# Low-rank decay and rate products of an RWKV-7 block: one cluster per token piece, the low-weight products on 64 rows each

## The chip, the cores and the metric

The kernel runs on one core of a Trainium2 chip. The metric is device time in microseconds (us) of one execution; of three executions of the kernel before, the median is 1004.59 us (1003.79 to 1004.99). Engines are named as the profile names them: PE is TensorE's matrix multiply, PEld its weight load, DVE is VectorE, ACT is ScalarE, POOL is GpSimd, SP issues most transfers.

## The reference, cut to what matters

One layer of a hybrid block works on 528 tokens (16 learned ones ahead of 512 real ones) of width 2048. One input projection has 65 tiles of 128 columns; they feed an RWKV-7 branch of 16 heads and a short convolution branch, and one output projection joins both. One of the 65 tiles holds two low-rank inputs of 64 columns: `wl` for the decay and `al` for the rate.

```python
Pr = Pr + (prev - Pr) * mu_shift[l]          # token shift
wl = Pr[..., 4*D_RWKV : 4*D_RWKV + 64]
al = Pr[..., 4*D_RWKV + 64 :]
w_raw = -softplus(-(w0[l] + tanh(wl) @ w_lora_up[l])) - 0.5
decay = exp(-exp(w_raw))
a = sigmoid(a0[l] + al @ a_lora_up[l])       # per channel, 1024 wide
```

Decay and rate enter the recurrence over time of every head. The kernel computes them for a pair of heads (128 channels) at a time, so there are eight pairs.

## The kernel before, in words

**Number format.** Products run in a rounded 32-bit form (`F32R`), and a 32-bit operand is split in two: a high part, which is a copy in that form, and a low part, which is the rest. A full product is high by high, high by low and low by high.

**The input projection as filler.** `mains` (from L493) is a generator that emits the projection's matmuls (L346) tile by tile, in the order of `plan`. Everything else is placed among them: `fill(ns)` (L564) draws projection matmuls until their estimated time has passed, then the next piece of other work is emitted. The order of PE's instructions is this order, written out by hand; on the other engines a planner orders them by estimated times and priorities. A projection weight comes by a transfer on SP (L166), is cast on ACT (L158) and its low part is made on DVE or POOL (L159).

**A pair.** `prepare(i)` (L640) does one pair: it loads and splits the pair's low-rank weights (`lora_up`, L602; `luh` high, `lul` low, each 128 rows by 2 by 128), calls `low_rank` for the decay argument `tz` (index 0) and then for the rate argument `ta` (index 1), and goes on to a running sum `cc` (L654), two exponentials `e` (L656, L658), the operands `ar` and `bk` (L661 to L678) and the matmuls `gram` (L694). Pairs are taken two at a time; after the second, `invert` solves a small triangular system for both.

**The low-rank input `la`.** `use_lora` (L395) makes it once: for each of the two inputs, rows 0 to 63 hold the high part and rows 64 to 127 the low part. The weights come from the host twice over, in rows 0 to 63 and again in rows 64 to 127. So one matmul of 128 rows, `hi[:, j]` by `la[:, j]`, gives the high weights times high and low part of the input together.

**`low_rank` (L578).** For each of two pieces of the tokens (0 to 272, and 272 to 528) it takes one PSUM bank from a pool of two (`pz`, tag `tz`, which `gram` and `invert` use as well), issues a matmul with the high weights (L584) and one with the low weights (L585), both over 128 rows, then one or two ACT instructions that apply tanh out of the bank (L588 and L589 for the first piece, L591 for the second), and calls `fill(FW["lora"])`, 2200 ns of projection matmuls. The order on PE for a pair is thus: decay piece 1, filler, decay piece 2, filler, rate piece 1, filler, rate piece 2, filler.

**Later.** The recurrence over nine chunks (`recur`, from L953) uses what is left of the projection as filler; then comes the output projection (L1256).

Of the kernel before, what the change touches and what calls it, by code (L numbers as in the profile page):

```python
# [9 lines left out]
F32 = mybir.dt.float32  # L10
F32R = mybir.dt.float32r
I32 = mybir.dt.int32
AF = mybir.ActivationFunctionType
ALU = mybir.AluOpType
# [4 lines left out]
P = 128  # L19
# [3 lines left out]
META = 16  # L23
L = SEQ + META
CH = 64
NCH = SEQ // CH + 1
LP = NCH * CH
# [15 lines left out]
FW = dict(  # L43
    evac=34, start=1062, lora=2200, gram=8000, gram_b=13500, gram2=5500, misc=2000, v=2000, vt=1000, solve=24500, more={0: 5500, 2: 2400},
    tr=3200, lev=3000, cp=4200, out=1500, begin=19500, p=2900, u=2900, s=5200, last=3700, mix=2600,
)
# [52 lines left out]
def hymba_kernel(ctx: ExitStack, tc: tile.TileContext, xt, xtok, front, w_in, w_out, pv, lup, cst, msk, gf, out):  # L99
    nc = tc.nc  # L100
# [18 lines left out]
    def col(off, i=0):  # L119
        return pvt[:, off + i : off + i + 1]  # L120
# [59 lines left out]
    la = cq.tile([P, 2, L], F32R, name="la")  # L180
    ones = xp.tile([P, P + 2], F32R, name="ones")
    omm = xp.tile([P, 33], F32, name="omm")
    hv = xp.tile([P, 6, 8], F32, name="hv")
# [3 lines left out]
    pz = ph1.enter_context(tc.tile_pool(name="pz", bufs=2, space=PSUM))  # L187
# [6 lines left out]
    def tr(name, dt=F32):  # L194
        return cq.tile([P, LP], dt, tag="tr", name=name, bufs=5)

    def tm(name):
        return tp.tile([P, LP], F32, tag="tm", name=name, bufs=3)
# [118 lines left out]
    with tc.issue_after(head):  # L317
        nc.vector.tensor_scalar(
            out=omm, in0=pvt[:, V_MU : V_MU + 33], scalar1=-1.0, scalar2=1.0, op0=ALU.mult, op1=ALU.add
        )  # L320
        for d, off in (
# [4 lines left out]
                out=d, in0=pvt[:, off : off + 8], scalar1=0.5, scalar2=None, op0=ALU.mult  # L326
            )
        nc.vector.tensor_scalar(
            out=hv[:, 4], in0=pvt[:, V_KA : V_KA + 8], scalar1=-0.5, scalar2=1.0, op0=ALU.mult, op1=ALU.add
# [37 lines left out]
    def shift_full(ps, m, name, dst):  # L367
        pr = tp.tile([P, L + 1], F32, tag="pr", name=f"pr_{name}", bufs=2)
        nc.gpsimd.memset(pr[:, 0:1], 0.0)
        scaled(FULL, ps, pr, -1)  # L370
        sh = tm(f"sh_{name}")[:, 0:L]
        nc.scalar.activation(sh, pr[:, 0:L], AF.Copy, scale=col(V_MU, m))
        for (a, b), d in dst:
            nc.vector.scalar_tensor_tensor(
                out=d, in0=pr[:, a + 1 : b + 1], scalar=omm[:, m : m + 1], in1=sh[:, a:b], op0=ALU.mult, op1=ALU.add
            )
# [13 lines left out]
    def gate(g, name):  # L390
        th = tm(f"th_{name}")[:, 0:SEQ]
        nc.scalar.activation(th, g, AF.Tanh, scale=0.5)
        nc.vector.scalar_tensor_tensor(out=g, in0=th, scalar=1.0, in1=g, op0=ALU.add, op1=ALU.mult)

    def use_lora(ps):  # L395
        pre = tm("lora_pre")[:, 0:L]
        shift_full(ps, 32, "lora", (((0, L), pre),))
        th = tr("lora_th")[0:64, 0:L]
        al = tr("lora_al")[0:64, 0:L]
        nc.scalar.activation(th, pre[0:64], AF.Tanh)  # L400
        nc.vector.tensor_copy(al, pre[64:128])
        for j, t in enumerate((th, al)):
            nc.scalar.copy(la[0:64, j], t)
            nc.vector.tensor_tensor(out=la[64:128, j], in0=t, in1=la[0:64, j].bitcast(F32), op=ALU.subtract)

    got = {}

# [3 lines left out]
    def use(what, i, ps):  # L411
        if what == "lora":
            use_lora(ps)
        elif what in ("k", "v"):
            t = cq.tile([P, LP], F32, tag=what, name=f"{what}{i}")
# [139 lines left out]
    def step():  # L555
        t = next(flow, None)
        if t is None:
            run_pending(float("inf"))
        else:
            clock[0] += t  # L560
            run_pending(clock[0])
        return t

    def fill(ns):  # L564
        while ns > 0:
            seen = len(ready)
            t = step()
            if t is None:
                return
            ns -= t  # L570
            if len(ready) > seen:
                ns += FW["evac"]
# [2 lines left out]
        while key not in ready:  # L575
            step()

    def low_rank(i, j, up, w0, name, pad):  # L578
        t = tr(name)
        nc.gpsimd.memset(t[:, META:CH], pad)  # L580
        hi, lo = up
        for a, b in ((0, 272), (272, L)):
            z = pz.tile([P, b - a], F32, tag="tz", name=f"{name}_{a}")
            nc.tensor.matmul(z, hi[:, j], la[:, j, a:b], start=True, stop=False)  # L584
            nc.tensor.matmul(z, lo[:, j], la[:, j, a:b], start=False, stop=True)  # L585
            with tc.high_priority(offset=AHEAD):
                if a == 0:
                    nc.scalar.activation(t[:, 0:META], z[:, 0:META], AF.Tanh, bias=w0, scale=0.5)  # L588
                    nc.scalar.activation(t[:, CH : 5 * CH], z[:, META:272], AF.Tanh, bias=w0, scale=0.5)  # L589
                else:  # L590
                    nc.scalar.activation(t[:, 5 * CH : LP], z, AF.Tanh, bias=w0, scale=0.5)  # L591
            fill(FW["lora"])
        return t


    def ahead():
# [2 lines left out]
    def c3(t):  # L599
        return t.rearrange("p (c s) -> p c s", s=CH)  # L600

    def lora_up(i):  # L602
        raw = cq.tile([P, 2, P], F32, tag="lur", name=f"lur{i}")
        hi = cq.tile([P, 2, P], F32R, tag="luh", name=f"luh{i}")
        lo = cq.tile([P, 2, P], F32R, tag="lul", name=f"lul{i}")
        nc.sync.dma_start(raw, lup[i])
        nc.scalar.copy(hi, raw)
        nc.vector.tensor_tensor(out=lo, in0=raw, in1=hi.bitcast(F32), op=ALU.subtract)
        return hi, lo

    def split(t, name, n):
# [2 lines left out]
        nc.scalar.copy(hi, t)  # L614
        nc.vector.tensor_tensor(out=lo, in0=t, in1=hi.bitcast(F32), op=ALU.subtract)
        return hi, lo

    heads = [(h, slice(64 * h, 64 * h + 64), slice(64 - 64 * h, 128 - 64 * h)) for h in range(2)]

    place = [(i % 2) * 4 + i // 2 for i in range(NPAIR)]  # L620
    dd = keep.tile([P, NCH, NPAIR], F32, name="dd")
# [18 lines left out]
    def prepare(i):  # L640
# [6 lines left out]
        up = lora_up(i)  # L647
        fill(FW["start"] if i else 6700)

        tz = low_rank(i, 0, up, hv[:, 0, i : i + 1], f"tz{i}", -1.0)  # L650
        ta = low_rank(i, 1, up, hv[:, 1, i : i + 1], f"ta{i}", 0.0)
        nc.gpsimd.tensor_scalar(out=tz, in0=tz, scalar1=1.0, scalar2=None, op0=ALU.add)
        cc = tr(f"cc{i}")
        nc.vector.tensor_tensor_scan(cc, smask.rearrange("p c s -> p (c s)"), tz, 0.0, op0=ALU.mult, op1=ALU.add)  # L654
# [8 lines left out]
            out=bk[:, :, 0], in0=c3(k), scalar=hv[:, 2, i : i + 1], in1=c3(te), op0=ALU.mult, op1=ALU.mult  # L663
# [3 lines left out]
            out=ta, in0=ta, scalar1=hv[:, 3, i : i + 1], scalar2=hv[:, 4, i : i + 1], op0=ALU.mult, op1=ALU.add  # L667
        )
        nc.vector.scalar_tensor_tensor(
            out=ar[:, :, 0], in0=c3(k), scalar=col(V_KK, i), in1=e1[:, :, 0:CH], op0=ALU.mult, op1=ALU.mult  # L670
# [8 lines left out]
            out=ar[:, 1:NCH, 1], in0=c3(r), in1=e1[:, 1:NCH, 1 : CH + 1], op=ALU.mult  # L679
        )  # L680
        nc.vector.scalar_tensor_tensor(
            out=r, in0=r, scalar=hv[:, 5, i : i + 1], in1=ta[:, CH:LP], op0=ALU.mult, op1=ALU.mult
# [41 lines left out]
        zs = ((zn, 0, 288), (ze[0][0:2, P : P + 288], 288, LP))  # L724
# [54 lines left out]
        def sub(x, r0, c0, dims):  # L779
            return bass.AP(tensor=x.tensor, offset=x.offset + r0 * 16 + c0, ap=[list(x.ap[0])] + dims)  # L780

        for m in (2, 4, 8):
            for b in range(16 // (2 * m)):
# [4 lines left out]
                    out=pq,  # L788
                    in0=sub(d, o, o + m, [[16, m], [0, m], [1, m]]),
                    in1=sub(y, o + m, o + m, [[0, m], [1, m], [16, m]]),  # L790
                    op=ALU.mult,
                )
                nc.vector.tensor_reduce(
                    out=tq.rearrange("p (i j) -> p i j", i=m), in_=pq, op=ALU.add, axis=AX.X
                )
                nc.vector.tensor_tensor(
                    out=pq,
                    in0=sub(y, o, o, [[16, m], [0, m], [1, m]]),
                    in1=bass.AP(tensor=tq.tensor, offset=tq.offset, ap=[list(tq.ap[0]), [0, m], [1, m], [m, m]]),
                    op=ALU.mult,  # L800
# [274 lines left out]
    for i in range(0, NPAIR, 2):  # L1075
        invert([prepare(i), prepare(i + 1)])
# [155 lines left out]
    def here(t, n):  # L1232
        return xa[t][:, n * 512 : (n + 1) * 512] if n < 2 else xb[n - 2][:, t]
# [99 lines left out]
    for half in range(2):  # L1333
        o = 28 * half
        for g in range(4):
            b = o + 4 + 4 * g
# [50 lines left out]
    z = {}  # L1387
# [55 lines left out]
    with tc.manual_schedule(engines={mybir.EngineType.DVE, mybir.EngineType.Activation, mybir.EngineType.Pool}):  # L1443
# [16 lines left out]
        for part in range(2):  # L1460
            cols = slice(256 * part, 256 * part + 256)
            for jj in range(8):
                hi, lo = right[(1, "M2", jj // 2), jj % 2]
# [4 lines left out]
            h = here(1, 2)[:, cols]  # L1468
# [70 lines left out]
```

## Time and profile before

| what | value |
|---|---|
| median of three executions | 1004.59 us |
| profiled execution, its own time | 1003.5 us |
| its span, first to last instruction | 1001.6 us |
| granted TensorE clock, mean | 0.997 of full speed |
| PE busy | 991.5 us (99%) |
| DVE, ACT, POOL busy | 679.7, 394.5, 273.2 us |
| low-rank matmuls | 64 (8 pairs, 2 inputs, 2 pieces, 2 weight parts) |

A row of the timeline gives the start, the time, the engine, the line, what is written and read, the array tile (rows by columns, as in 128\*128), the moving operand's shape and how many like instructions were merged in the row. Matmuls are pipelined: a duration of 0.28 us is the time until a result is out, while the next matmul starts about 0.12 us after. What a matmul costs in a dense stream is therefore the distance from its start to the next start. The rows "PEld" are weight loads, which run beside the matmul before them.

### The profile page before, as it was taken

To read this page: it belongs to the slowest core of one execution; us is meant where nothing else is said; L and a number is where in the kernel's file an instruction comes from. 1 tells how busy PE (TensorE), PEld (TensorE's weight loads), DVE (VectorE), ACT (ScalarE), POOL (GpSimd) and SP (SyncE) were. 2 spreads that over 40 slices of the span, in tenths; PEclk is the share of its full clock that TensorE was granted. 3 is DMA by queue.
4 is the path that set the end of the run, shared out by engine and by line. 5 is a ranking of instruction groups with operands and counts; after the bars stand their busy time and mean duration, and the time that the engine had idled before them with its cause. 6 is when DMAs were issued, how large, how long until landed. Compare 5 with 4: busy or idle time off the path is not lost.

```text
span 1001.6 us, 23672 instructions
## 1 busy us (share of the span) xinstructions
PE 991.5 (99%) x9723; PEld 913.1 (91%) x9723; DVE 679.7 (68%) x1247; ACT 394.5 (39%) x729; POOL 273.2 (27%) x284
## 2 busy tenths in 40 slices
PE   9999999999999999999999999999999999999996
PEld 8999999999998999998999998989889898888885
DVE  7777865586775569654669654245555697997897
ACT  7553423344323434322434322223232435546454
POOL 0122524234222423233423232223332333001001
PEclk9999999999999999999999999999999999999998
DMA  9426586546675364854263855868674698797654
GB/s 332 144 84 152 126 219 159 153 128 143 154 185 168 99 167 101 216 158 119 85 173 96 224 143 166 321 201 249 203 227 101 171 268 212 187 304 188 160 127 168
DMA packets 185036, 174.82 MB, mean 175 GB/s; under 512 B 121568, under 2 KB 142816, under 8 KB 184416
## 3 DMA queue, kind: packets, MB, share of 16 engines
q1 hardware_dynamic: 182336, 164.40, 56.8%
q0 software_dynamic: 2304, 8.39, 4.9%
q8 instruction: 76, 1.25, 0.5%
q10 hardware_dynamic: 288, 0.52, 0.1%
q14 instruction: 32, 0.26, 0.1%
HBM read 136.92 MB, written 36.35 MB: 173 GB/s over the span
## 4 chain that ended last, share of the span: by engine, by line
PE 95%; DVE 3%; issue 1%; DMA 0%; ACT 0%; DVEq 0%; POOL 0%; ACTq 0%
PE ps_k L346 9%; PE ps_v L346 9%; PE ps_h L346 9%; PE ps_r L346 9%; PE ps_C L346 9%; PE ps_g L346 9%; PE ps_B L346 9%; PE ps_gc L346 9%; PE M L1256 5%; PE P L1256 4%; PE g L694 2%; PE Q L1256 2%; DVE o L1227 1%; PE ps_lora L346 1%; PE zs L1019 1%; PE rz L967 1%
## 5 line engine op out<-in xcount | busy, mean ns | idle before, releaser
L159 POOL TENSOR_TENSOR w<-wr,w 128x512 fp32r<-128x512 f32 x119 | 173.1, 1455 | 367.5 <-ACT w L158 316.3
L158 ACT CAST w<-wr 128x512 fp32r<-128x512 f32 x252 | 153.1, 619 | 287.2 <-PE ps_C L346 48.9
L159 DVE TENSOR_TENSOR w<-wr,w 128x512 fp32r<-128x512 f32 x133 | 98.2, 744 | 107.8 <-ACT w L158 107.5
L346 PE MATMUL ps_k<-xh,w 128*128 128x272 f32 (+1 forms) x512 | 95.3, 284 | 0.0
L346 PE MATMUL ps_v<-xh,w 128*128 128x256 f32 (+1 forms) x512 | 95.3, 284 | 0.0
L346 PE MATMUL ps_r<-xh,w 128*128 128x258 f32 (+1 forms) x512 | 94.9, 281 | 0.0
L346 PE MATMUL ps_h<-xh,w 128*128 128x256 f32 (+1 forms) x512 | 94.2, 283 | 0.0
L346 PE MATMUL ps_C<-xh,w 128*128 128x256 f32 (+1 forms) x512 | 93.1, 281 | 0.0
L346 PE MATMUL ps_g<-xh,w 128*128 128x256 f32 (+1 forms) x512 | 91.5, 280 | 0.0
L346 PE MATMUL ps_B<-xh,w 128*128 128x512 f32 x256 | 83.9, 395 | 0.0
L346 PE MATMUL ps_gc<-xh,w 128*128 128x512 f32 x256 | 81.3, 392 | 0.0
L346 PEld LDWEIGHTS ps_k<-xh,w 128*128 128x128 f32 x512 | 80.0, 188 | 0.4
L346 PEld LDWEIGHTS ps_v<-xh,w 128*128 128x128 f32 x512 | 80.0, 188 | 0.3
L346 PEld LDWEIGHTS ps_h<-xh,w 128*128 128x128 f32 x512 | 79.3, 188 | 0.9 <-issue 0.2
L346 PEld LDWEIGHTS ps_r<-xh,w 128*128 128x128 f32 x512 | 79.9, 188 | 0.1
L346 PEld LDWEIGHTS ps_C<-xh,w 128*128 128x128 f32 x512 | 79.2, 188 | 0.6
L346 PEld LDWEIGHTS ps_g<-xh,w 128*128 128x128 f32 x512 | 78.7, 188 | 0.3
L346 PE MATMUL ps_k<-xl,w 128*128 128x272 f32 (+1 forms) x256 | 72.6, 284 | 0.0
L346 PE MATMUL ps_v<-xl,w 128*128 128x272 f32 (+1 forms) x256 | 72.5, 283 | 0.0
L346 PE MATMUL ps_r<-xl,w 128*128 128x258 f32 (+1 forms) x256 | 72.2, 282 | 0.0
L346 PE MATMUL ps_g<-xl,w 128*128 128x258 f32 (+1 forms) x256 | 72.0, 281 | 0.0
L346 PE MATMUL ps_C<-xl,w 128*128 128x258 f32 (+1 forms) x256 | 71.8, 280 | 0.0
(321 smaller groups left out, 2256.7 us busy)
## 6 DMA issues: line engine op xcount, KB each, us to landing
wr<-in_w_in_dram SPq DMA_DIRECT2D x126, 512.0 KB
ct<-opd SPq DMA_DIRECT2D x64, 288.0 KB
wo<-in_w_out_dram SPq DMA_DIRECT2D x24, 512.0 KB
x<-in_w_out_dram POOLq DMA_DIRECT2D x16, 512.0 KB, 6.1
opd<-ar SPq DMA_DIRECT2D x8, 576.0 KB
opd<-gt SPq DMA_DIRECT2D x16, 288.0 KB
opd<-bt SPq DMA_DIRECT2D x64, 64.0 KB
x<-in_w_out_dram SPq DMA_DIRECT2D x8, 512.0 KB
```

Source lines behind the costliest of these rows:

```text
L158: nc.scalar.copy(hi, rq)
L159: low[q] = eng.tensor_tensor(out=lo, in0=rq, in1=hi.bitcast(F32), op=ALU.subtract).ins
L346: nc.tensor.matmul(ps[r], ww[:, w], xx[:, kt, a:b], start=(kt == 0 and n == 0), stop=(kt == KT - 1 and n == 2))
L694: nc.tensor.matmul(z[h][:, c - c0], bk[hs, c, h : h + 2, :].rearrange("p a s -> p (a s)"), ar[hs, c].rearrange("p a s -> p (a s)"), start= ...
L967: nc.tensor.matmul(z[e][ho if e else hs, 0, k], t[hs, o : o + CH], t[hs, O_V : O_V + CH] if part else st[hs, 4 * e + k], start=(part == 0 ...
L1019: nc.tensor.matmul(d[hs, j], w, x[hs], start=(a == 0), stop=(a == b - 1))
L1227: last = nc.vector.tensor_tensor(out=lo, in0=rq, in1=hi.bitcast(F32), op=ALU.subtract)
L1256: nc.tensor.matmul(bank[s], left(prod, jj, m, s), w, start=(jj == 0 and n == 0), stop=(jj == 7 and n == 2))
```

## The change

`low_rank` is called once for a pair and handles both inputs. For each piece of the tokens it takes two banks at once, one for decay and one for rate. It issues the two matmuls with the high weights, over 128 rows as before, and then the two with the low weights, now over 64 rows each and against the high part of the input alone: decay on rows 0 to 63, rate on rows 64 to 127 (the product of the two low parts is no longer formed). For that, `use_lora` stores the rate's high part in rows 64 to 127 and its low part in rows 0 to 63, the other way round than the decay's. The ACT instructions of both inputs follow the cluster, and one `fill` of twice 2200 ns. `heads`, which lists the two halves of rows (index, own half, other half), is defined earlier.

```diff
@@ use_lora
         for j, t in enumerate((th, al)):
-            nc.scalar.copy(la[0:64, j], t)
-            nc.vector.tensor_tensor(out=la[64:128, j], in0=t, in1=la[0:64, j].bitcast(F32), op=ALU.subtract)
+            nc.scalar.copy(la[heads[j][1], j], t)
+            nc.vector.tensor_tensor(out=la[heads[j][2], j], in0=t, in1=la[heads[j][1], j].bitcast(F32), op=ALU.subtract)
@@ low_rank
-    def low_rank(i, j, up, w0, name, pad):
-        t = tr(name)
-        nc.gpsimd.memset(t[:, META:CH], pad)
+    def low_rank(i, up):
         hi, lo = up
+        both = [tr(f"{n}{i}") for n in ("tz", "ta")]
+        for t, pad in zip(both, (-1.0, 0.0)):
+            nc.gpsimd.memset(t[:, META:CH], pad)
         for a, b in ((0, 272), (272, L)):
-            z = pz.tile([P, b - a], F32, tag="tz", name=f"{name}_{a}")
-            nc.tensor.matmul(z, hi[:, j], la[:, j, a:b], start=True, stop=False)
-            nc.tensor.matmul(z, lo[:, j], la[:, j, a:b], start=False, stop=True)
+            zs = [pz.tile([P, b - a], F32, tag="tz", name=f"{n}{i}_{a}") for n in ("tz", "ta")]
+            for j, z in enumerate(zs):
+                nc.tensor.matmul(z, hi[:, j], la[:, j, a:b], start=True, stop=False)
+            for (j, hs, ho), z in zip(heads, zs):
+                nc.tensor.matmul(z, lo[hs, j], la[hs, j, a:b], start=False, stop=True)
             with tc.high_priority(offset=AHEAD):
-                if a == 0:
-                    nc.scalar.activation(t[:, 0:META], z[:, 0:META], AF.Tanh, bias=w0, scale=0.5)
-                    nc.scalar.activation(t[:, CH : 5 * CH], z[:, META:272], AF.Tanh, bias=w0, scale=0.5)
-                else:
-                    nc.scalar.activation(t[:, 5 * CH : LP], z, AF.Tanh, bias=w0, scale=0.5)
-            fill(FW["lora"])
-        return t
+                for j, (t, z) in enumerate(zip(both, zs)):
+                    w0 = hv[:, j, i : i + 1]
+                    if a == 0:
+                        nc.scalar.activation(t[:, 0:META], z[:, 0:META], AF.Tanh, bias=w0, scale=0.5)
+                        nc.scalar.activation(t[:, CH : 5 * CH], z[:, META:272], AF.Tanh, bias=w0, scale=0.5)
+                    else:
+                        nc.scalar.activation(t[:, 5 * CH : LP], z, AF.Tanh, bias=w0, scale=0.5)
+            fill(2 * FW["lora"])
+        return both
@@ prepare
-        tz = low_rank(i, 0, up, hv[:, 0, i : i + 1], f"tz{i}", -1.0)
-        ta = low_rank(i, 1, up, hv[:, 1, i : i + 1], f"ta{i}", 0.0)
+        tz, ta = low_rank(i, up)
```

More of the change, by code (lines that the diff above doesn't have):

```diff
@@ L393, in gate @@
         nc.vector.scalar_tensor_tensor(out=g, in0=th, scalar=1.0, in1=g, op0=ALU.add, op1=ALU.mult)
+    heads = [(h, slice(64 * h, 64 * h + 64), slice(64 - 64 * h, 128 - 64 * h)) for h in range(2)]
     def use_lora(ps):
@@ L616, in split @@
         return hi, lo
-    heads = [(h, slice(64 * h, 64 * h + 64), slice(64 - 64 * h, 128 - 64 * h)) for h in range(2)]
     place = [(i % 2) * 4 + i // 2 for i in range(NPAIR)]
```

## The prediction

> **What bounds the kernel now.** I read the page first (busy times and the chain that ended last), then PE's own waits.
>
> ```profile
> span 1001.6 us, 23672 instructions
> PE 991.5 (99%) x9723; PEld 913.1 (91%) x9723; DVE 679.7 (68%) x1247; ACT 394.5 (39%) x729; POOL 273.2 (27%) x284
> ...
> PE 95%; DVE 3%; issue 1%; DMA 0%; ACT 0%; DVEq 0%; POOL 0%; ACTq 0%
> ```
> ```profile
> PE pwarm L207 <- DVE cold L204: 1.4, 1, 1.4
> PE M L1256 <- DVE o L1227: 0.5, 1, 0.5
> ```
>
> PE carries 95% of the chain, and in the whole execution it waits twice, for 1.9 us together, neither time near the low-rank work. So whatever is added to or taken from PE's stream moves the end by as much, and the other engines matter only if they come late. The question is what a cluster costs on PE, in start-to-start distances.
>
> **What is removed: half of the low-weight matmuls' time.** The groups of the low-rank matmuls by their operand `la`, then the timeline of PE at the decay's two pieces of the first pair and the rate's second:
>
> ```profile
> L584 PE MATMUL tz<-la,luh x16: 278/286/293, 60.0 to 522.7; 128*128 128x272 f32 x8, 128*128 128x256 f32 x8
> L585 PE MATMUL tz<-la,lul x16: 277/285/296, 60.2 to 522.8; 128*128 128x272 f32 x8, 128*128 128x256 f32 x8
> L584 PE MATMUL ta<-la,luh x16: 280/284/291, 65.3 to 527.9; 128*128 128x272 f32 x8, 128*128 128x256 f32 x8
> L585 PE MATMUL ta<-la,lul x16: 280/286/293, 65.5 to 528.0; 128*128 128x272 f32 x8, 128*128 128x256 f32 x8
> ```
> ```profile
> 60.04 0.29 PE L584 MATMUL tz<-la,luh 128*128 128x272 f32 x1
> 60.17 0.29 PE L585 MATMUL tz<-la,lul 128*128 128x272 f32 x1
> 60.30 0.42 PE L346 MATMUL ps_v<-xh,w 128*128 128x272 f32 x2
> ...
> 62.72 0.28 PE L584 MATMUL tz<-la,luh 128*128 128x256 f32 x1
> 62.84 0.28 PE L585 MATMUL tz<-la,lul 128*128 128x256 f32 x1
> 62.96 0.29 PE L346 MATMUL ps_v<-xl,w 128*128 128x272 f32 x1
> ...
> 68.03 0.28 PE L584 MATMUL ta<-la,luh 128*128 128x256 f32 x1
> ```
>
> A matmul of 272 columns takes 0.13 us of the stream (60.04, 60.17, 60.30), one of 256 columns 0.12. They sit in the stream without a gap, their weight loads hidden. There are 16 pairs of low-weight matmuls (8 head pairs by 2 pieces). If the two of a pair run side by side, each pair costs one instead of two: 8 x 0.13 + 8 x 0.12 = 2.0 us off.
>
> **What is added: a switch of the array to 64 rows and back, 16 times.** The kernel has one place where a block of 64\*128 matmuls stands in the 128\*128 stream: `gram`. Its timeline, the long block (16 matmuls, two records each, so 32) and the short one (4 records):
>
> ```profile
> 78.94 0.28 PE L346 MATMUL ps_r<-xl,w 128*128 128x256 f32 x1
> 79.05 0.39 PE L346 MATMUL ps_r<-xh,w 128*128 128x256 f32 x2
> 79.37 2.06 PE L694 MATMUL g<-ar,bk 64*128 64x128 f32 x32
> 81.35 0.38 PE L346 MATMUL ps_r<-xl,w 128*128 128x256 f32 x1
> 81.58 0.40 PE L346 MATMUL ps_r<-xh,w 128*128 128x256 f32 x2
> ```
> ```profile
> 87.15 0.28 PE L346 MATMUL ps_r<-xl,w 128*128 128x256 f32 x1
> 87.27 0.28 PE L346 MATMUL ps_r<-xh,w 128*128 128x256 f32 x1
> 87.48 0.49 PE L694 MATMUL g<-ar,bk 64*128 64x128 f32 x4
> 87.90 0.29 PE L726 MATMUL n<-sq_h,ones 128*2 128x288 f32 x1
> ```
> ```profile
> 120.85 0.38 PE L694 MATMUL g<-ar,bk 64*128 64x128 f32 x2
> ```
> ```profile
> 87.15 0.19 PEld L346 LDWEIGHTS ps_r<-xh,w 128*128 128x128 f32 x1
> 87.47 0.30 PEld L694 LDWEIGHTS g<-ar,bk 64*128 64x128 f32 x4
> ```
>
> First, side by side is real: two records fit in 0.38 us, the time of one. Long less short block: (81.35 - 79.37) - (87.90 - 87.48) = 1.98 - 0.42 = 1.56 us for 14 more twos of records, 0.111 us each. Then the price of the switch:
> - Going in, the first start comes 0.21 us after the last 128-row one (87.27 to 87.48) where 0.12 is the step (87.15 to 87.27): 0.09 lost.
> - The short block takes 0.42 us, of which two twos are 0.22: 0.20 lost inside. The weight loads show it: that of the last `ps_r` matmul starts at 87.15, ahead of its matmul at 87.27, but that of `g` only at 87.47, with its matmul. Nothing is loaded ahead over the switch.
> - Coming out, the first 128-row matmul lasts 0.38 instead of 0.28 (81.35): 0.10, its own load in the open.
>
> Together 0.39 us for each visit to 64 rows, and 16 x 0.39 = 6.2 us.
>
> Is it the rows, or that `gram`'s operands are plain 32-bit while the low-rank ones are rounded? The nearest row with plain 32-bit operands on 128 rows:
>
> ```profile
> 49.91 0.40 PE L346 MATMUL ps_B<-xl,w 128*128 128x512 f32 x1
> 50.15 0.39 PE L346 MATMUL ps_B<-xh,w 128*128 128x512 f32 x1
> 50.38 0.60 PE L487 MATMUL prs<-cs,yb 128*128 128x128 f32 x4
> ```
>
> There the format changes at 50.38 with no delay: 0.23 us after the one before, as between 49.91 and 50.15 (0.24). So I charge the rows. Nothing in the trace shows rounded operands on 64 rows. From below, the pair might run like the 128-row stream with no switch cost (0); from above, two visits' worth if the halves did not share one visit (0.78). I take 0.39, since `gram` has the same tile, the same two halves and two banks.
>
> A rule to weigh: in the Trainium skill, "TensorEngine Tiling (Array Packing)", section "Tiling Modes", says that changing the tiling mode drains the array; that speaks against this change, and the late weight loads above agree with it. That page gives no price, but "TensorE: Matmul & The Clock Gate" puts a drain at about 128 cycles (section "Step-by-step: what each phase is for") and a load of 128 columns at 128/1.2 ns (section "LDWEIGHTS (loading the stationary operand)"). As an estimate from that page, a visit is 2 x (53 + 107) ns = 0.32 us, and the sum would be about +3.1 us instead of +4.2; the trace's 0.39 decides.
>
> **The sum.** +6.2 - 2.0 = +4.2 us. The profiled execution (1003.5 us, span 1001.6 with 1.9 around it) would become 1007.7. The median of the three runs is 1.1 above it, so the forecast in their terms is 1004.59 + 4.2 = **1008.8 us**.
>
> **What costs nothing, and its cover.** The filler per pair is the same in sum (4 x 2200 ns or 2 x 4400); matmuls only change places, and the projection's total is fixed. ACT, DVE, POOL and SP issue the same instructions with the same shapes, in a partly different order. Three covers are thinner, and each has its row (DVE's timeline, then PE's):
>
> ```profile
> 58.52 0.70 DVE L404 TENSOR_TENSOR la<-lora_al,la 64x528 fp32r<-64x528 f32 x1
> ...
> 75.65 1.85 DVE L673 TENSOR_TENSOR bk<-ta,e 128x576 f32<-128x576 f32 x1
> ...
> 190.01 2.42 DVE L931 COPY xT<-z 32x128 f32<-32x128 f32 x8 [0.56 <-PE z L925]
> ```
> ```profile
> 192.92 0.29 PE L584 MATMUL tz<-la,luh 128*128 128x272 f32 x1
> 193.05 0.29 PE L585 MATMUL tz<-la,lul 128*128 128x272 f32 x1
> ```
>
> - The rate's half of `la` is written at 59.22 and now read at 60.17 with the first cluster, not at 65.3: 0.95 us to spare.
> - The decay's second piece moves from 62.72 to about 60.04 + 0.76 + 40 matmuls x 0.12 = 65.6, that is 2.9 us later, and with it `tz`, `cc` and `e`. But `te` also needs the rate, whose last piece was at 68.03 and now comes with it at 65.7; so the later of the two inputs comes no later. The end of this branch is `bk` at 77.50, against `gram` at 79.37: 1.9 us of cover, more by the 0.5 us net that the two visits put ahead of `gram`.
> - Two banks are wanted at once. For the third pair the second bank is freed by `invert`'s copies at 192.43, and its first use moves to 193.05: 0.6 us of cover where there were 3.
>
> **The rivals.**
>
> *A, no switch cost: faster.* Rounded operands on 64 rows flow in the stream and only the 2.0 us is left: 1002.6 us, at -0.2% just on the edge of what a measurement of this kernel tells from no change. It decides wherever a visit costs under 2.0/16 = 0.125 us. For it: side by side is shown. Against it: both blocks of `gram` pay 0.39. This would be the outcome by "TensorE: Matmul & The Clock Gate", section "Part 3: Packing small matmuls — row/col tiling", in the Trainium skill, whose recipe puts small products in distinct row groups and counts only some 4 ns for each added tile. Chance 5%.
>
> *D, half of it.* One crossing of the two is hidden because a 64-row load may go ahead, or the matmul behind it is long enough to cover its own: 16 x 0.195 - 2.0 = +1.1 us, 1005.7, no change. Against it: the load at 87.47. Chance 7%.
>
> *B, the change does not do what it says.* The two low matmuls run one after the other and the 2.0 us is not saved: +6.2 us, 1010.8. Against it: the two records in 0.38 us. Chance 7%.
>
> *C, a new wait on top.* The order on DVE and ACT shifts around the weights' splits, where PE is already late once:
>
> ```profile
> 297.69 0.39 PE L346 MATMUL ps_B<-xl,w 128*128 128x512 f32 x1
> 298.10 0.74 PE L346 MATMUL ps_B<-xh,w 128*128 128x512 f32 x2
> ```
>
> That step is 0.41 us instead of 0.23 (the low half of a weight came late): 0.18 us a time. A few of these, or the third pair's bank, would give +0.5 to +1.5: about 1009.8. Chance 17%.
>
> **How the numbers follow.** The forecast has the remaining 64%, with its own range 1008.0 to 1009.4 (a visit at 0.34 to 0.43, the three runs' spread of 1.2). The range 1006.8 to 1011.0 takes in C and B, and a visit of 0.27 as its low end; A and D, 12%, lie outside. Faster by over 0.2%: A, 0.05. Within 0.2%: D, 0.07. Slower: the rest, 0.88.
>
> **What the changed profile would show.** At each cluster on PE: two 128\*128 matmuls of `la`, a step of about 0.21 to the 64\*128 pair, the pair's two records starting together, and about 0.43 from the pair's start to the next projection matmul, whose duration is some 0.10 longer than its neighbours'. Per cluster 0.76 us from its first start to that matmul's effective start, against 0.25 + 0.25 before. `gram` and the bank uses show no wait. The prediction is wrong if the weight loads of the low pair start while a 128-row matmul before them still streams, if the pair's records start 0.12 apart, or if PE's waits list new lines worth more than 0.5 us.

## The result and the profile after

The changed kernel takes 1008.62 us (median of five executions, 1008.47 to 1009.62), the kernel before 1003.79 us (1003.50 to 1004.99) beside it: 4.83 us more, a ratio of 1.0048 (95% interval 1.0038 to 1.0059). The profiled execution's span is 1006.9 us against 1001.6.

First the busy times and the chain from the page of the changed kernel, then its waits of PE (for whom, by which line; us in total, times, longest):

```profile
span 1006.9 us, 23677 instructions
PE 995.9 (99%) x9723; PEld 912.8 (91%) x9723; DVE 683.4 (68%) x1247; ACT 395.8 (39%) x729; POOL 265.6 (26%) x284
...
PE 94%; DVE 3%; issue 1%; DMA 1%; SPq 0%; POOL 0%; ACT 0%; DVEq 0%; ACTq 0%
```
```profile
PE pwarm L207 <- DVE cold L204: 1.4, 1, 1.4
PE ps_h L346 <- issue: 0.7, 1, 0.7
PE M L1260 <- DVE o L1231: 0.5, 1, 0.5
PE t L870 <- DVE xn L861: 0.2, 1, 0.2
```

PE still carries 94% of the chain and has as many matmuls as before, 9723, but is busy 4.4 us longer. Two waits are new: one of 0.2 us in `invert` and one of 0.7 us, "issue", in which PE waits for nothing that the profile shows. The timeline of PE at the two clusters of the first pair, with the groups of the low-rank matmuls:

```profile
60.17 0.29 PE L588 MATMUL tz<-la,luh 128*128 128x272 f32 x1
60.30 0.29 PE L588 MATMUL ta<-la,luh 128*128 128x272 f32 x1
60.52 0.39 PE L590 MATMUL tz<-la,lul 64*128 64x272 f32 x1
60.52 0.39 PE L590 MATMUL ta<-la,lul 64*128 64x272 f32 x1
60.84 0.52 PE L346 MATMUL ps_v<-xh,w 128*128 128x272 f32 x2
61.19 0.29 PE L346 MATMUL ps_v<-xl,w 128*128 128x272 f32 x1
...
65.59 0.28 PE L588 MATMUL tz<-la,luh 128*128 128x256 f32 x1
```
```profile
L588 PE MATMUL tz<-la,luh x16: 279/285/292, 60.2 to 530.0; 128*128 128x272 f32 x8, 128*128 128x256 f32 x8
L590 PE MATMUL tz<-la,lul x16: 380/384/389, 60.5 to 530.3; 64*128 64x272 f32 x8, 64*128 64x256 f32 x8
L590 PE MATMUL ta<-la,lul x16: 381/386/389, 60.5 to 530.3; 64*128 64x272 f32 x8, 64*128 64x256 f32 x8
```

The two low products start together (60.52), 0.22 us after the high one where 0.13 is the step, and the matmul behind them starts 0.32 us later (60.84) and is followed after 0.35 us by the third (61.19), two steps. In a stream without a gap those two steps would be 0.25, so the cluster takes (61.19 - 0.25) - 60.17 = 0.77 us, where four matmuls of 128 rows took 4 x 0.127 = 0.51: 0.26 more, 16 times, is 4.2 us. All 32 low products are alike: 0.38 to 0.39 us each, where they had 0.28 and 0.29.

The rest of the 5.3 us between the two spans is in waits. The `gram` groups of before and of after (number of records, ns minimum/median/maximum, first and last start), then the timeline of PE at the fifth pair's `gram`, before and after:

```profile
L694 PE MATMUL g<-ar,bk x288: 272/272/373, 79.4 to 553.9; 64*128 64x128 f32 x144
```
```profile
L698 PE MATMUL g<-ar,bk x288: 272/272/373, 79.7 to 558.9; 64*128 64x128 f32 x144
...
  DVE ar L682: 0.3, 2
```
```profile
351.28 0.71 PE L694 MATMUL g<-ar,bk 64*128 64x128 f32 x8
```
```profile
354.16 0.95 PE L698 MATMUL g<-ar,bk 64*128 64x128 f32 x8
```

Eight records that took 0.71 us take 0.95: `gram` waits there, and once more in the seventh pair, for DVE's `ar`. By the start of the last `gram` matmul the changed kernel is 558.9 - 553.9 = 5.0 us behind: 4.2 of clusters, twice 0.24, and the 0.2 in `invert`. After that only the "issue" wait is to come. A second measure for the runs below lies ahead of that wait: the distance from the first low-rank matmul to the last `gram` matmul. It begins at the first low-rank matmul because the runs reach that one at different times, from 59.7 to 60.5 us among the kernels with the new order, before PE's work differs. In the kernel before it is 553.9 - 60.0 = 493.9 us, in the changed one 558.9 - 60.2 = 498.7, 4.8 more.

### The profile page after: what moved, and what is told of

Same layout as the page of the kernel before. It is cut to its first block, busy times and chain, and to the rows that moved or that the text cites. A ratio compares the mean times of both kernels' runs of the same rounds, so it can differ in the third digit from the quotient of the medians.

```text
span 1006.9 us, 23677 instructions
## 1 busy us (share of the span) xinstructions
PE 995.9 (99%) x9723; PEld 912.8 (91%) x9723; DVE 683.4 (68%) x1247; ACT 395.8 (39%) x729; POOL 265.6 (26%) x284
## 3 DMA queue, kind: packets, MB, share of 16 engines
q8 instruction: 76, 1.25, 0.5%
## 4 chain that ended last, share of the span: by engine, by line
PE 94%; DVE 3%; issue 1%; DMA 1%; SPq 0%; POOL 0%; ACT 0%; DVEq 0%; ACTq 0%
PE ps_v L346 9%; PE ps_r L346 9%; PE ps_h L346 9%; PE ps_C L346 9%; PE ps_g L346 9%; PE ps_B L346 9%; PE ps_k L346 9%; PE ps_gc L346 8%; PE M L1260 5%; PE P L1260 4%; PE g L698 2%; PE Q L1260 2%; DVE o L1231 1%; PE ps_lora L346 1%; PE zs L1023 1%; PE zy L1027 1%
## 5 line engine op out<-in xcount | busy, mean ns | idle before, releaser
L159 POOL TENSOR_TENSOR w<-wr,w 128x512 fp32r<-128x512 f32 x119 | 168.8, 1419 | 377.3 <-ACT w L158 323.6
L346 PE MATMUL ps_h<-xl,w 128*128 128x258 f32 (+1 forms) x256 | 71.8, 281 | 0.7 <-issue 0.7
```

The lines of the kernel that those rows point to most:

```text
L159: low[q] = eng.tensor_tensor(out=lo, in0=rq, in1=hi.bitcast(F32), op=ALU.subtract).ins
L346: nc.tensor.matmul(ps[r], ww[:, w], xx[:, kt, a:b], start=(kt == 0 and n == 0), stop=(kt == KT - 1 and n == 2))
```

## The experiments

**The theory** was the prediction's: a visit to 64 rows costs PE 0.39 us, whoever makes it, and the saved halves give 2.0 us back. **The rivals**: the new order (two inputs in one cluster, one filler for both) costs the time and not the rows; or the pair is not really side by side.

**1. The new order with 128 rows.** The changed kernel with the low products over all rows:

```diff
-            for (j, hs, ho), z in zip(heads, zs):
-                nc.tensor.matmul(z, lo[hs, j], la[hs, j, a:b], start=False, stop=True)
+            for j, z in enumerate(zs):
+                nc.tensor.matmul(z, lo[:, j], la[:, j, a:b], start=False, stop=True)
```

> The cluster and everything around it stay as changed, but both low-weight products run over 128 rows again. Theory (the visit to 64 rows costs 0.39 us on PE, 16 times): the 4.2 us go and only the waits of the new order are left, so +0.0 to +1.0 us against the kernel before, 1003.8 to 1004.8. Rival (the cluster's order, its two banks at once and the later decay are what costs): still about +4.8 us, 1008.6. A middle value would share the loss between them.

1005.95 us against 1003.88 of the kernel before, ratio 1.0018 (1.0009 to 1.0026). More than half of the loss is gone with the rows, but 2.1 us stay, over the 0.9 at most that the theory had left for the order. The group of `gram` with what line L698 waited for (us, times), then the timeline of PE at the fifth pair:

```profile
L698 PE MATMUL g<-ar,bk x288: 272/272/373, 79.5 to 555.8; 64*128 64x128 f32 x144
...
  DVE ar L682: 1.3, 4
```
```profile
352.20 0.49 PE L698 MATMUL g<-ar,bk 64*128 64x128 f32 x4
352.93 1.83 PE L698 MATMUL g<-ar,bk 64*128 64x128 f32 x28 [0.24 <-DVE ar L682]
354.69 0.40 PE L346 MATMUL ps_v<-xh,w 128*128 128x272 f32 x1
```

The row counts each wait twice, once at the matmul and once at its weight load: there are two, in the fifth and the seventh pair. Each costs 0.5 us, since the block takes 354.69 - 352.20 = 2.49 us where an undisturbed one takes 1.98. The last `gram` matmul starts 1.9 us later than before (555.8 against 553.9). Of that, 0.5 lies ahead of the first low-rank matmul (60.5 against 60.0), where PE waits 0.5 and 0.2 us for ACT's and DVE's first operands. The distance is 1.4 us longer: 1.0 in the two waits for `ar`, and 0.4 in places that I did not take apart. So the order alone costs something, and the question is what of it.

**2. The filler split one to three.** In the changed kernel, and in the kernel of experiment 1, the second piece is brought closer to the first, with the same filler in sum:

```diff
-            fill(2 * FW["lora"])
+            fill((1 if a == 0 else 3) * FW["lora"])
```

> As changed, but the second cluster of a pair comes after 2200 ns of filler instead of 4400 (the other 6600 follow it). Theory (part of the loss is that the decay is finished later, so that the operand ar reaches gram late in the fifth and seventh pair): the two waits of 0.24 us go, the 16 visits stay: 1008.1, about 0.5 us under the changed kernel. Rival (the waits come from elsewhere): no difference, 1008.6, and the waits still stand in the trace.

> As e1_full_rows (clusters, but low products over 128 rows), with the second cluster after 2200 ns of filler. Theory: the two waits of gram for ar (0.5 us each in e1_full_rows) go, so 1.0 us under it: 1005.0, and what is left above the kernel before is the wait of invert's first matmuls (0.4) and the late instruction fetch. Rival (the cluster's order costs in another way): still 1006.

With 64 rows 1008.18 us (ratio 1.0040, 1.0028 to 1.0053), with 128 rows 1003.94 us (ratio 1.0002, 0.9993 to 1.0011), against 1003.97; the second is 1.1 us under what was expected. The groups of `gram` in both, 64 rows first:

```profile
L698 PE MATMUL g<-ar,bk x288: 272/272/373, 79.4 to 557.7; 64*128 64x128 f32 x144
```
```profile
L698 PE MATMUL g<-ar,bk x288: 272/272/373, 79.5 to 553.9; 64*128 64x128 f32 x144
```

| low products | filler one to one | filler one to three |
|---|---|---|
| on 64 rows | 1008.62 (+4.8) | 1008.18 (+4.0) |
| on 128 rows | 1005.95 (+1.4) | 1003.94 (-0.4) |

(Medians, and in brackets the distance from the first low-rank matmul to the last `gram` matmul, against 493.9 us in the kernel before.) Three things follow. With the second piece sooner, the new order costs nothing: its 2.0 us (1.8 by the distance) were a late second piece. In that column only the rows differ, and they cost 4.24 us by the medians, 4.4 by the distance; with the 2.0 us that are saved, a visit costs 0.39 or 0.40 us. And in the first column the two costs do not add: on 64 rows the late piece costs 0.44 by the medians and 0.8 by the distance, not 2.0, since PE, held up by the visits, comes later to what it would have waited for. The medians also hold the "issue" wait, which is 0.7 us in the changed kernel's profile and 1.2, 1.2 and 1.7 in those of the other three, so their differences are less sure than the distances.

**3. The number of visits.** One change gathers both pieces of a pair in one cluster, four high and then four low products, with 8 visits instead of 16 (the second piece takes two banks of another pool):

```diff
-            for (j, hs, ho), z in zip(heads, zs):
+        for (a, b), zz in zip(cuts, zs):
+            for (j, hs, ho), z in zip(heads, zz):
...
-            fill(2 * FW["lora"])
+        fill(4 * FW["lora"])
```

> One cluster per pair instead of two: four high products, then the four low ones of 64 rows, then the filler of all 8800 ns; the second piece's banks come from the other pool. 8 visits instead of 16. Theory: 8 x 0.39 - 2.0 = +1.1 us against the kernel before, and no late decay, so 1004.9 (1004.4 to 1005.6). Rival (the cost goes with the number of 64-row matmuls, which stays 32, not with the visits): +4.2 us, 1008.

The other goes back to the order before and puts each low product alone on 64 rows: 32 visits and nothing saved (as in the changed kernel, the product of the two low parts is left out):

```diff
-            nc.tensor.matmul(z, lo[:, j], la[:, j, a:b], start=False, stop=True)
+            nc.tensor.matmul(z, lo[0:64, j], la[0:64, j, a:b], start=False, stop=True)
```

> The kernel before in its order, but every low-weight product runs on rows 0 to 63 alone (its product with the low part of the input is left out), so 32 visits and no partner beside. Theory: 32 x 0.39 = +12.5 us, 1016.3. Rival (order): no order changes, so about +0 us, 1003.8. Rival (a visit costs what its pair costs, not the switch): half of the change's switch cost per visit, about +6, 1010.

8 visits: 1004.97 us, +1.09 (ratio 1.0011, 1.0003 to 1.0020). 32 visits: 1015.68 us, +11.8 (ratio 1.0119, 1.0105 to 1.0133), 0.37 each. By the distance they are +0.6 and +12.1. The second is the dearest of all and has the order, the filler and, but for one of 0.2 us, the waits of the kernel before. Its timeline of PE at the first visit:

```profile
60.13 0.29 PE L584 MATMUL tz<-la,luh 128*128 128x272 f32 x1
60.35 0.39 PE L585 MATMUL tz<-la,lul 64*128 64x272 f32 x1
60.67 0.52 PE L346 MATMUL ps_v<-xh,w 128*128 128x272 f32 x2
61.03 0.29 PE L346 MATMUL ps_v<-xl,w 128*128 128x272 f32 x1
```

0.22 us in and 0.32 out, as in the changed kernel. With 8, 16 and 32 visits, and 2.0, 2.0 and 0 us saved, 0.39 a visit gives +1.1, +4.2 and +12.5; measured +1.1, +4.2 (experiment 2) and +11.8. The number of 64-row products is 32 in all three, so the cost goes with the visits and not with the products.

**4. One after the other.** The changed kernel with both low products on rows 0 to 63, so that the pair can't run side by side (`use_lora` is as in the kernel before, with the rate's high part in these rows):

```diff
-                nc.tensor.matmul(z, lo[hs, j], la[hs, j, a:b], start=False, stop=True)
+                nc.tensor.matmul(z, lo[0:64, j], la[0:64, j, a:b], start=False, stop=True)
```

> As changed, but both low-weight products lie on rows 0 to 63, so they cannot run side by side. Theory: the visit costs the same and the second product is paid, 16 x 0.125 = +2.0 us on top of the changed kernel, 1010.6. Rival (side by side never saved anything): the same as the changed kernel, 1008.6.

1010.12 us, 1.5 over the changed kernel (ratio to before 1.0064, 1.0050 to 1.0078). The low products of the first cluster:

```profile
60.00 0.39 PE L590 MATMUL tz<-la,lul 64*128 64x272 f32 x1
60.23 0.29 PE L590 MATMUL ta<-la,lul 64*128 64x272 f32 x1
60.45 0.52 PE L346 MATMUL ps_v<-xh,w 128*128 128x272 f32 x2
```

They start 0.23 us apart instead of together, and the matmul behind them 0.22 after the second instead of 0.32: 0.13 us more a cluster (0.12 with 256 columns), 2.0 in all. By the distance it is 1.7 (+6.5 against +4.8). Some 0.2 of the rest is hidden, because the two waits of `gram` for `ar` cost 0.13 us each here instead of 0.24. So side by side saves what the prediction took, and the rival falls.

**5. What the low products cost altogether.** The kernel before without them (the low parts of the low-rank weights are left out of the computation):

```diff
-            nc.tensor.matmul(z, hi[:, j], la[:, j, a:b], start=True, stop=False)
-            nc.tensor.matmul(z, lo[:, j], la[:, j, a:b], start=False, stop=True)
+            nc.tensor.matmul(z, hi[:, j], la[:, j, a:b], start=True, stop=True)
```

> The kernel before in its order without any low-weight product (the low parts of the low-rank weights are left out), so 32 matmuls of 128 rows fewer and no visit to 64 rows. Theory (a matmul in the stream costs its start-to-start distance, 0.13 or 0.12 us): 32 x 0.124 = -4.0 us, 999.8 to 999.9. Rival (the other engines or transfers come late when PE runs ahead): the gain is smaller, about 1002.

It came out at 1004.99 us, no faster than before (ratio 1.0010, 1.0001 to 1.0019), although its last `gram` matmul starts at 549.4, 4.5 us ahead. The time goes in the recurrence, where PE's waits have a new line, and PE's timeline the row:

```profile
PE zy L1022 <- issue: 3.8, 2, 2.5
```
```profile
654.85 0.21 PE L1022 MATMUL zy<-st,ct 64*64 64x64 f32 x1 [2.53 <-issue]
```

Counted in the trace's records of PE (matmuls, weight loads, semaphores), the two waits stand at the 12737th and the 14785th. The "issue" wait of the kernel before and of the changed one stands at the 16833rd in both, 0.16 and 0.88 us (start to start, less the usual step; the view of waits counts 0.7 of the second). These places differ by 2048 and by 4096, whole multiples of 256. The instructions come by a DMA queue of their own, with the same row on the pages of the kernel before and of this one:

```profile
q8 instruction: 76, 1.25, 0.5%
```

76 packets for 1.25 MB are some 16 KB each, and PE's 19537 records in the kernel before are 257 for each packet. That gave a theory: the waits come where one block of PE's instructions ends and the next is late, and leaving out matmuls had moved these places into the recurrence's densest stretches of small matmuls. Two kernels move the places alone. To the kernel without low products, 16 matmuls of one column (64 instructions) are added at the start, which brings the places back to where they were; to the kernel before, 48 of them (192 instructions), which brings them to where they are in the kernel without low products:

```diff
+    for _ in range(16):
+        nc.tensor.matmul(pwarm[0:16, 0:1], cold[:, 0:16], cold[:, 0:1], start=True, stop=True)
```

> The kernel without the products of the low weights (that part of the reference's work is left out), and 16 matmuls of one column more at the start: 64 instructions on TensorE, which bring every later instruction of its stream back to the place that it has in the kernel before. If the stalls of 2.75 and 1.46 us without a wait in the kernel without low products hang on where a block of TensorE's instructions ends, both go, and the 4.0 us of the saved products come out: 999.9, and up to 1.2 us for the added matmuls, 999.9 to 1001.1. If they hang on the transfers or on the recurrence being reached sooner, they stay: 1005.0 to 1006.2.

> The kernel before, all its work done, and 48 matmuls of one column more at the start: 192 instructions, so that the stream of TensorE stands to its blocks of 256 as it does in the kernel without low products. If the stalls hang on where a block ends, stalls without a wait of some 2.7 and 1.5 us come in at the recurrence, beside up to 3.6 us for the added matmuls: 1007.9 to 1011.5. If not, only the added matmuls show: 1004.2 to 1007.4.

With 16 added, 1000.12 us (ratio 0.9961, 0.9948 to 0.9973): more instructions, and 4.9 us less. With 48 added, 1013.03 us (ratio 1.0091, 1.0075 to 1.0106) against 1004.00. PE's waits for "issue", of the first and of the second:

```profile
PE ps_h L348 <- issue: 0.2, 1, 0.2
```
```profile
PE zy L1025 <- issue: 3.9, 2, 2.7
```

The first is back at the 16833rd record; the second's waits stand at the 12993rd, 14273rd and 15041st, all at the same place in a block of 256. Up to the last `gram` the second is 3.1 us behind the kernel before, all of it ahead of the first low-rank matmul, and 9.1 at its end; the growth lies in the recurrence, between its first long wait at 660 us and its last at 717. The waits are not the whole of it. After the first one the granted clock of PE falls, as the stretch from 663 to 667 us shows (us, PE busy and matmuls, granted clock, DMA share, GB/s), and with it the matmuls of 512 columns slow down:

```profile
663.00:667.00 4.00, 4.00 (x19) 0.57 1.00 382
```
```profile
664.48 1.05 PE L348 MATMUL ps_B<-xh,w 128*128 128x512 f32 x2
665.34 0.63 PE L348 MATMUL ps_B<-xl,w 128*128 128x512 f32 x1
...
668.33 0.62 PE L348 MATMUL ps_gc<-xh,w 128*128 128x512 f32 x2
668.78 0.39 PE L348 MATMUL ps_gc<-xl,w 128*128 128x512 f32 x1
```

Two of them take 0.86 us of the stream (664.48 to 665.34) and, once the clock is back, 0.45 (668.33 to 668.78). In the same stretch the kernel before has a granted clock of 1.00. Eight steps of 0.43 us instead of 0.23 are 1.6 us, about what the median lies above the most that the theory had said (1.5). Part of the 3.1 us at the start is of the same kind: from 8 to 12 us the granted clock is 0.57, against 1.00 before. The profile of the kernel without low products shows no such fall, but its eleven executions have mean granted clocks of 0.994 to 0.998, against 0.997 to 0.999 in the kernel before, so some of its loss may be clock as well.

That the place decides is shown; that the next block is late is what fits (each wait ends 1.3 to 1.6 us after the end of the instruction transfer ahead of it), and no run varied the transfers. Nor does the place alone settle the length: at the 16833rd record the wait is between 0.2 and 1.7 us in the profiles here. The kernel with 16 added beats both, at the price of the low parts of these weights.

## Why the prediction was right

**The price of a visit, and the sum: right.** Forecast +4.2, measured +4.83 by the medians and +5.3 by the spans, inside the range. `gram` was the right row: 0.39 us from plain 32-bit operands held for rounded ones. Of the shapes foreseen, the step to the pair is 0.22 (foreseen 0.21), the matmul behind it 0.39 us instead of 0.29 (0.10 longer), and the cluster 0.77 (0.76). Only the split inside was off: 0.32 instead of about 0.43 from the pair's start to the next start, with the 0.10 of that matmul coming on top, after it has started; the sum is the same. That 1008.62 stands even closer to the 1008.8 of the forecast is luck: beside it the kernel before took 1003.79 us, and not the 1004.59 from which the forecast set out.

**Rows, not format: right.** Experiments 1 and 2 keep operands, order and banks and change only the rows: 4.24 us. The prediction had argued it from the row of `prs`, which is of transposes (L487) and not of products; these runs show it.

**Side by side: right.** Records 0.00 apart, and 1.5 us when they may not be (B falls). In the Trainium skill, "TensorEngine Tiling (Array Packing)", section "Tiling Modes", has the array drain when the mode changes; both the late starts and the cost by number of visits agree. The prediction's estimate of 0.32 us a visit, from the Trainium skill's "TensorE: Matmul & The Clock Gate", sections "Step-by-step: what each phase is for" and "LDWEIGHTS (loading the stationary operand)", would have given +3.1; 0.37 to 0.40 was measured, so the trace's own row was the better price.

**A and D: wrong, as expected.** A needed a visit under 0.125 us, D 0.195. In the Trainium skill, "TensorE: Matmul & The Clock Gate", section "Part 3: Packing small matmuls — row/col tiling", counts about 4 ns for an added tile. Here the added tile did cost next to nothing (the pair's two starts together), but a pair in a stream of 128-row matmuls costs the visit, 0.26 us net of what it saves.

**"The later of the two inputs comes no later": wrong.** This is the step that failed. It asked when `tz` and `ta` are ready, and left out that the decay still has three steps to go on three engines before `te` can use it. Timeline of POOL, DVE and ACT in the changed kernel, fifth pair, up to `te`; then ACT and DVE in the kernel before:

```profile
341.17 1.83 POOL L656 TENSOR_SCALAR tz<-tz 128x576 f32<-128x576 f32 x1
343.04 1.36 DVE L658 TENSOR_TENSOR_SCAN cc<-smask,tz 128x576 f32<-128x576 f32 x1 [1.56 <-POOL tz L656]
345.02 0.67 ACT L662 ACTIVATE e<-cc 128x576 f32<-128x576 f32 x1
345.92 0.74 DVE L665 SCALAR_TENSOR_TENSOR te<-ta,e 128x576 f32<-128x576 f32 x1
```
```profile
339.87 0.68 ACT L658 ACTIVATE e<-cc 128x576 f32<-128x576 f32 x1
340.74 0.49 ACT L591 ACTIVATE ta<-ta,hv 128x256 f32<-128x256 f32 x1
341.26 0.76 DVE L661 SCALAR_TENSOR_TENSOR te<-ta,e 128x576 f32<-128x576 f32 x1
```

Before, `e` was done (340.55) before the rate's last piece (341.23): the decay's steps ran while PE made the rate. Now both inputs come together, and some 5 us of steps stand in the path. `te` moved by 4.66 us (341.26 to 345.92), `gram` by 2.88 (351.28 to 354.16): 1.8 us of cover are gone.

**"The end of this branch is `bk`, 1.9 us of cover": the wrong end and the wrong pair.** `ar` stands behind it in DVE's order, and the first pair is not the tightest. DVE's row before and after:

```profile
349.24 0.68 DVE L678 TENSOR_TENSOR ar<-r,e 128x512 f32<-128x512 f32 x1
```
```profile
353.88 0.68 DVE L682 TENSOR_TENSOR ar<-r,e 128x512 f32<-128x512 f32 x1
```

Before, it ended 1.36 us ahead of `gram` (349.92 against 351.28); after, 0.40 behind (354.56 against 354.16). That is the loss of 1.8 us again. "`gram` and the bank uses show no wait" was thus wrong for `gram` (two of 0.24 us) and right for the banks: no wait shows at the third pair's. The cost stayed at 0.4 to 0.8 us (experiment 2) only because the visits held PE back, which the prediction did not foresee: on 128 rows the same late piece costs 2.0. That the sum held in spite of this step was luck.

**C, a new wait on top: came in part.** It had +0.5 to +1.5 with a chance of 17%. The distance to the last `gram` and the spans put the extra at some 0.6 to 1.1 us: 0.5 at `gram`, 0.2 in `invert`, and 0.7 more at the "issue" wait (0.88 for 0.16), less a gap of 0.25 that the recurrence had before, at 630.6, and has no more. The median's +4.83 lies between the forecast and C, and by the runs' spread the two can't be told apart there. The bank and the weights' splits, which C named, were not the cause.

**The signs of being wrong.** Of the three that the prediction named, one came: PE's waits list two new lines, 0.7 and 0.2 us, together over 0.5. They come on top of the 4.2 us and do not replace them. The other two did not come: the pair's records start together, and its weight loads start with it, 0.22 us after the high product before them and so after the 0.13 us that this one takes of the stream. The row of the first of the two loads:

```profile
60.52 0.18 PEld L590 LDWEIGHTS tz<-la,lul 64*128 64x128 f32 x1
```

## What to carry to other kernels

In a stream of 128-row matmuls, packing small products on 64 rows pays only if one visit holds more than its own price: here 0.39 us, three matmuls of 272 columns, against one saved. Where two inputs are joined into one step, follow each to the operation that needs both, on every engine, and look at the pair with the least cover rather than the first. And a cover that the profile shows may be lent by the delay under study: the late second piece cost 2.0 us without the visits and 0.4 to 0.8 with them.

## What the runs showed of the hardware that was not expected

A stall of PE of up to 2.96 us, from one start to the next, without any wait in the program came and went with the number of PE's instructions ahead of it: 4.9 us were won by adding 16 matmuls of one column, and waits of 3.9 us brought in by adding 48. They stand at whole multiples of 256 records from each other, and were long only in the recurrence's stretches of 64x64 matmuls, some 0.03 us apart and less, or just behind one. After a stall of 2.96 us the granted clock was 0.57 over the next 4 us, which cost another 1.6. A difference of a few us between two kernels with different numbers of matmuls can be this alone. The changed kernel and the kernel before have the same 9723 matmuls, and the stall at the same place; it is still 0.7 us of the 5.3 between their spans.
